# The convolution of branch A started two units earlier with its norm behind it, and the residual for the memory stage rebuilt

## The chip, the cores and the metric

The kernel runs on one core of a Trainium2 chip. The metric is the time of one execution in device microseconds, from the first to the last instruction of that core with what lies around it. TensorE (PE; its weight loads are shown as PEld), VectorE (DVE), ScalarE (ACT), GpSimd (POOL) and the queue that issues the transfers (SP) run side by side, each through its own list of instructions in order.

## The reference, cut to what matters

One layer over 256 tokens of width 1024, in fp32:

```python
h = layer_norm(x, ln0_g, ln0_b)
z = h @ w_in + b_in                       # 13 parts: a_val, a_gate, b_*, c_*, d_*, g_merge
u = a_val * sigmoid(a_gate)                                   # branch A
y_a = silu(layer_norm(causal_depthwise_conv(u, conv_a_w, conv_a_b), ln_a_g, ln_a_b))
...                                       # y_b: gated linear attention, y_c: stick-breaking, y_d: RG-LRU
proj   = einsum("bsnc,ncd->bsnd", stack([y_a, y_b, y_c, y_d]), w_branch)
merged = sum(sigmoid(g_merge) * proj, over the four branches)
h = layer_norm(ALPHA * h + merged @ w_out + b_out, ln1)
h = layer_norm(ALPHA * h + cross_attention(h, mem), ln2)
h = layer_norm(ALPHA * h + moe(h), ln3)   # 32 experts, top 4, w1 1024x2048, w2 1024x1024 each
```

The convolution of branch A has 31 taps over 512 channels, so each token needs the 30 before it. Its norm runs over the 512 channels.

## The kernel before, in words

All weights of the layer ahead of the experts come as tiles of 1 MB, and each tile is one **unit** of work. A unit is loaded by a transfer that SP issues, split into a high part (cast by ACT, L162) and a low part (the remainder, 5/16 of it on POOL, L164, and 11/16 on DVE, L166), and multiplied on PE in three passes (high by high, high by low, low by high; L135, L137, L139). There are two raw buffers and three split ones, so a raw buffer is free for the next load when both parts of the low half are done, and the split of unit i+3 needs unit i to be done on PE. `step` issues one unit at a time and splits two units ahead.

Units are counted from 0 here. 0 to 3 are the value and gate of branch A; 4 to 9 the queries, keys and values of branch C (4 and 7 queries, 5 and 8 keys, 6 and 9 values); 10 to 19 are for branches B and D. Then come gates and branch projections, in the order of branches C, B, D, A: 20 to 25 for C, 26 to 31 for B (29 and 30 are gates, 28 and 31 projections), 32 to 37 for D, and for A the gates 38 to 41 and the projections 42 and 43. 44 is the first tile of `ca_wk` (keys of the memory), 45 to 48 are `w_out`.

What is not a unit is a **chain**: a generator that `advance` moves on twice in every step, once before the unit's first half and once before its second half. So what a chain issues stands in each engine's list at that place, and the list is fixed when the program is built. The chains that the change touches:

- `chain_conv`: the convolution, 124 taps on DVE (L377 the first of a block of 128 channels, L379 the others), each over 128 x 256 numbers in SBUF. It starts ahead of unit 4, two taps at each advance.
- `chain_a`: the norm of branch A. Sums over the channels on PE with a matrix of 1/512 (L389 `ps_am` the mean, L396 `ps_av` the variance), the rest on DVE and ACT, and last `ysplit(0, ca)`, which casts `y_a` to `yh[0]` on ACT (L128) and puts the remainder in `yl[0]` on DVE (L129). PE needs `yh[0]` and `yl[0]` in units 42 and 43. It is appended ahead of unit 38.
- `chain_mem`: loads the memory (1 MB), `x` again (1 MB) and three rows broadcast to all partitions (0.5 MB each), splits the memory for units 44 and on, and builds ALPHA * LN(x) + b_out in `h`, to which units 45 to 48 add their products. The normalization runs on DVE (L861), gain and bias on POOL (L862, L864), the last step on DVE (L868). It is also appended ahead of unit 38.

Two buffers hold `yh` and two `yl`, given out in the order of branches C, B, D, A; so `yh[0]` takes the one of branch B, which unit 31 reads last. The PSUM tiles of units 4 to 19 come from a pool of two: unit 6 needs that of unit 4, which DVE empties with L422 (`qc`), and unit 8 that of unit 6, emptied with L433 (`vc`).

Behind the units come attention to the memory, routing, and the experts (w1 and w2 are 12.6 MB each expert, 402.7 MB in all), whose loads run through the freed buffers.

## Time and profile before

| | |
|---|---|
| median of three runs | 1424.52 us (1424.35 to 1425.74) |
| the profiled execution | 1425.04 us, of which the span of the instructions is 1423.3 us |
| PE busy | 1261.5 us (89%) |
| DVE busy | 522.1 us (37%) |
| ACT busy | 314.4 us (22%) |
| POOL busy | 231.2 us (16%) |
| transfers | 482.04 MB, mean 339 GB/s |

All times below are microseconds from the start of the span. Shares of the whole span say little, since it has two parts: up to some 480 us the units and chains, and from there the experts. A row of a timeline gives start and duration of one group of equal instructions in a row, and in brackets how long the engine sat idle before it and which instruction released it.

### The profile page before, as it was taken

How to read it: one execution, taken by the hardware profiler on the slowest of the kernel's cores; microseconds unless marked ns; L12 is line 12 of the kernel's file. 1: busy time of each engine (PE TensorE's matmuls, PEld its weight loads, DVE VectorE, ACT ScalarE, POOL GpSimd, SP SyncE). 2: the span in 40 equal slices, each digit the busy share in tenths (PEclk: the TensorE clock that was granted, in tenths of full speed). 3: DMA queues.
4: the chain of work that ended last, by engine and by line, in shares of the span. 5: the costliest groups of instructions: out<-in, count | busy, mean ns of one | idle time of the engine just before them, and what ended most of it. 6: DMA issues, size and time to landing. Idle time of an engine off the chain costs nothing. (4 is left out here: it accounts for less than half of the span.)

```text
span 1423.3 us, 18504 instructions
## 1 busy us (share of the span) xinstructions
PE 1261.5 (89%) x7677; PEld 743.5 (52%) x7677; DVE 522.1 (37%) x814; ACT 314.4 (22%) x433; POOL 231.2 (16%) x143
## 2 busy tenths in 40 slices
PE   6999999989999999876999799799889987977764
PEld 6989898988999743321443343244244332322211
DVE  5587779977944621211121121111112211211113
ACT  4475574453643300000000000000000000000001
POOL 6233234559653200000000000000000000000000
PEclk9999999998999999998999999999999999998988
DMA  6353334566565999999999999999999999999995
GB/s 235 119 177 121 119 119 154 187 237 191 195 258 206 387 424 407 424 424 425 427 424 426 424 424 427 425 426 425 424 425 426 426 423 424 425 427 426 425 420 240
DMA packets 51979, 482.04 MB, mean 339 GB/s; under 512 B 7840, under 2 KB 8240, under 8 KB 10704
## 3 DMA queue, kind: packets, MB, share of 16 engines
q1 hardware_dynamic: 51888, 480.79, 82.8%
q8 instruction: 62, 1.02, 0.3%
q14 instruction: 29, 0.24, 0.0%
HBM read 479.72 MB, written 1.05 MB: 338 GB/s over the span
## 5 line engine op out<-in xcount | busy, mean ns | idle before, releaser
L1471 PE MATMUL ps_h<-w,xg 128*32 128x512 f32 (+2 forms) x2048 | 419.0, 640 | 69.7 <-DMA w<-in_moe_w 65.8
L1471 PEld LDWEIGHTS ps_h<-w,xg 128*32 128x32 f32 (+2 forms) x2048 | 132.7, 134 | 331.6 <-issue 217.5
L1534 PE MATMUL ps_y<-w,at 128*32 128x512 f32 (+2 forms) x1024 | 213.5, 628 | 36.3 <-DMA w<-in_moe_w 34.5
L1480 DVE TENSOR_SCALAR act<-ps_h 128x512 f32<-128x512 f32 (+1 forms) x36 | 24.7, 687 | 503.6 <-PE ps_h L1471 503.6
L164 POOL TENSOR_TENSOR w_hl<-w_f,w_hl 128x640 fp32r<-128x640 f32 (+1 forms) x64 | 160.9, 2518 | 228.5 <-ACT w_hl L162 214.3
L1676 POOL TENSOR_TENSOR r<-r,gb 128x512 f32<-128x512 f32 x2 | 3.0, 1491 | 923.4 <-ACT r L1675 923.4
L1534 PEld LDWEIGHTS ps_y<-w,at 128*32 128x32 f32 (+2 forms) x1024 | 62.7, 133 | 165.5 <-issue 84.8
L166 DVE TENSOR_TENSOR w_hl<-w_f,w_hl 128x1408 fp32r<-128x1408 f32 x63 | 118.6, 1885 | 70.6 <-ACT w_hl L162 69.5
L162 ACT CAST w_hl<-w_f 128x2048 fp32r<-128x2048 f32 x63 | 119.9, 1905 | 104.6 <-DMA w_f<-in_w_in 35.2
L1518 ACT COPY ta<-ps_sc 128x256 f32<-128x256 f32 x31 | 11.6, 373 | 453.5 <-PE ps_sc L1516 453.5
L379 DVE SCALAR_TENSOR_TENSOR convacc<-u,cols,convacc 128x256 f32<-128x256 f32 x120 | 89.7, 747 | 2.5
L135 PE MATMUL ps_mm<-hT_hi,w_hl 128*128 128x256 f32 x512 | 75.5, 291 | 5.2 <-ACT hT_hi L311 2.1
L139 PE MATMUL ps_mm<-hT_hi,w_hl 128*128 128x256 f32 x512 | 73.1, 286 | 2.6 <-POOL w_hl L164 1.9
L137 PE MATMUL ps_mm<-hT_lo,w_hl 128*128 128x256 f32 x512 | 73.9, 288 | 0.0
L135 PEld LDWEIGHTS ps_mm<-hT_hi,w_hl 128*128 128x128 f32 x512 | 67.5, 195 | 8.2 <-issue 3.1
L1552 PE MATMUL acc<-y,ta 64*128 64x512 f32 (+1 forms) x248 | 69.3, 611 | 1.3
L139 PEld LDWEIGHTS ps_mm<-hT_hi,w_hl 128*128 128x128 f32 x512 | 67.0, 194 | 3.2 <-POOL w_hl L164 2.3
L137 PEld LDWEIGHTS ps_mm<-hT_lo,w_hl 128*128 128x128 f32 x512 | 67.6, 196 | 0.6 <-DVE hT_lo L314 0.6
L1342 PEld LDWEIGHTS ps_g<-sg,h 128*128 128x128 f32 x416 | 53.0, 207 | 13.1 <-issue 9.1
L1342 PE MATMUL ps_g<-sg,h 128*128 128x128 f32 x416 | 55.5, 295 | 0.3
L1481 ACT ACTIVATE sg<-act 128x512 f32<-128x512 f32 (+1 forms) x36 | 22.7, 631 | 134.8 <-DVE act L1480 134.2
L1541 ACT COPY y<-ps_y 128x512 f32<-128x512 f32 x28 | 16.4, 587 | 160.7 <-PE ps_y L1534 160.7
(398 smaller groups left out, 1246.9 us busy)
## 6 DMA issues: line engine op xcount, KB each, us to landing
w<-in_moe_w SPq DMA_DIRECT2D x128, 2048.0 KB, 29.4
w<-in_moe_w SPq DMA_DIRECT2D x128, 1024.0 KB, 29.5
w_f<-in_w_in SPq DMA_DIRECT2D x36, 1024.0 KB, 4.9
w_f<-in_w_branch SPq DMA_DIRECT2D x8, 1024.0 KB, 4.9
w_f<-in_ca_wk SPq DMA_DIRECT2D x4, 1024.0 KB, 5.0
w_f<-in_w_out SPq DMA_DIRECT2D x4, 1024.0 KB, 5.0
w_f<-in_ca_wq SPq DMA_DIRECT2D x4, 1024.0 KB, 5.0
w_f<-in_ca_wv SPq DMA_DIRECT2D x4, 1024.0 KB, 5.1
```

The lines of the kernel that those rows point to most:

```text
L135: PE.matmul(out, wh(i), xh(i), start=first and i == ks[0], stop=False)
L137: PE.matmul(out, wh(i), xl(i), start=False, stop=False)
L139: PE.matmul(out, wl(i), xh(i), start=False, stop=last and i == ks[-1])
L162: A.copy(hi, self.raw)
L164: G.tensor_tensor(lo[:, :n], self.raw[:, :n], hi.bitcast(F32)[:, :n], ALU.subtract)
L166: V.tensor_tensor(lo[:, n:], self.raw[:, n:], hi.bitcast(F32)[:, n:], ALU.subtract)
L379: V.scalar_tensor_tensor(ca[:, c, :], u[:, c, j:j + T], col("caw", 4 * j + c), ca[:, c, :], ALU.mult, ALU.add)
L1342: PE.matmul(pss[k // 4][:, k % 4 * w:(k % 4 + 1) * w], h[:, n, feature_tile(0, k)], sg[:, n, :w], start=n == 0 and k % 4 == 0, stop=n == N ...
L1471: PE.matmul(up_out(cap, hp_, m, i), x[:, k, :], w[:, c:c + 512], start=False, stop=k == KD - 1, skip_group_check=True)
L1480: V.tensor_scalar(g, hg, LIMIT, None, ALU.min)
L1534: PE.matmul(o, at[:, k, :], w[:, q * 512:(q + 1) * 512], start=k < (2 if cap == 32 else 1), stop=k >= KD - (2 if cap == 32 else 1), skip_g ...
L1552: PE.matmul(acc[n][q], a, b, start=False, stop=last, skip_group_check=True)
```

## The change

Three parts. The convolution starts ahead of unit 2, four taps at each advance until unit 7 and two from there, and `chain_a` follows as soon as the taps are issued; its last step waits, when the program is built, until unit 31 has been issued. The residual is built with `c0 = ALPHA * b0 + b_out` (one DVE step) and per token tile `(x - mean) * g0` and `* (ALPHA * rstd) + c0` (two DVE steps), with nothing on POOL. The transfers of `chain_mem` are issued at three advances, between weight loads, instead of one.

```diff
-    taps_per_step = 2
-
     def chain_conv():
...
-                if n % taps_per_step == 0:
+                if n >= (4 if st_["done"] < 7 else 2):
+                    n = 0
                     yield
+        yield from chain_a()
...
+        while not (wb_done and 3 in yh):
+            yield
         ysplit(0, ca)
...
+            if (n, hf) == (1, 1):
+                wb_done.append(1)
...
     chains.append(chain_b0())
+    conv[0] = chain_conv()
+    chains.append(conv[0])
     until(4)
     pms[:] = [(pmm, "mm")]
-    conv[0] = chain_conv()
-    chains.append(conv[0])
     until(7)
...
     def chain_mem():
         S.dma_start(mf, t["memT"])
+        yield
         S.dma_start(h, xrow)
-        g0, b0, bo = bcast("ln0_g"), bcast("ln0_b"), bcast("b_out")
+        g0 = bcast("ln0_g")
         for q in range(4):
-            yield
             yield
             sl = slice(2 * q, 2 * q + 2)
             split(mf[:, sl, :], mTh[:, sl, :], mTl[:, sl, :])
-            if q < 2:
-                V.tensor_scalar(h[:, q, :], h[:, q, :], *mr0[q], ALU.subtract, ALU.mult)
-                G.tensor_tensor(h[:, q, :], h[:, q, :], g0, ALU.mult)
+            yield
+            if q == 0:
+                b0 = bcast("ln0_b")
+                c0 = bcast("b_out")
+            elif q < 3:
+                n = q - 1
+                mean, rstd = mr0[n]
+                V.scalar_tensor_tensor(h[:, n, :], h[:, n, :], mean, g0, ALU.subtract, ALU.mult)
+                V.tensor_scalar(rstd, rstd, ALPHA, None, ALU.mult)
             else:
-                G.tensor_tensor(h[:, q - 2, :], h[:, q - 2, :], b0, ALU.add)
-        yield
+                V.scalar_tensor_tensor(c0, b0, ALPHA, c0, ALU.mult, ALU.add)
         for n in range(NT):
             yield
-            V.scalar_tensor_tensor(h[:, n, :], h[:, n, :], ALPHA, bo, ALU.mult, ALU.add)
+            V.scalar_tensor_tensor(h[:, n, :], h[:, n, :], mr0[n][1], c0, ALU.mult, ALU.add)
...
-    chains.append(chain_a())
     chains.append(chain_mem())
```

What this does to the lists of the engines is shown at three places. The first is DVE from the low part of unit 3 to `qc`, which empties the PSUM tile of unit 4. `u` is the input of the convolution (L276), `lr`, `e1`, `b16` and `e3` belong to branch B, and the `w_hl` tiles are the low parts of the weights. Before:

```order
L129 TENSOR_TENSOR wlr_lo_191<-wlr_190,wlr_hi_192 128x128
L166 TENSOR_TENSOR w_hl_359<-w_f_295,w_hl_359 128x1408
L505 TENSOR_SCALAR lr_437<-ps_lr_412,cols_82 16x256
L166 TENSOR_TENSOR w_hl_441<-w_f_357,w_hl_441 128x1408
L276 SCALAR_TENSOR_TENSOR u_198<-ps_mm_363,cols_82,a_sg_494 128x256 x2
L513 TENSOR_SCALAR e1_211<-ps_ga_499,cols_82 128x256 x2
L377 TENSOR_SCALAR convacc_200<-u_198,cols_82 128x256
L379 SCALAR_TENSOR_TENSOR convacc_200<-u_198,cols_82,convacc_200 128x256
L166 TENSOR_TENSOR w_hl_512<-w_f_439,w_hl_512 128x1408
L379 SCALAR_TENSOR_TENSOR convacc_200<-u_198,cols_82,convacc_200 128x256 x2
L422 TENSOR_SCALAR qc_204<-ps_mm_516,cols_82 128x256 x2
```

The same place of the changed kernel, from the first taps on (its lines 376 and 378 are the taps, 277 is `u`, 509 and 517 are `lr` and `e1`, 426 is `qc`):

```order
L376 TENSOR_SCALAR convacc_200<-u_198,cols_82 128x256
L378 SCALAR_TENSOR_TENSOR convacc_200<-u_198,cols_82,convacc_200 128x256 x3
L166 TENSOR_TENSOR w_hl_363<-w_f_295,w_hl_363 128x1408
L378 SCALAR_TENSOR_TENSOR convacc_200<-u_198,cols_82,convacc_200 128x256 x4
L509 TENSOR_SCALAR lr_445<-ps_lr_420,cols_82 16x256
...
L166 TENSOR_TENSOR w_hl_453<-w_f_361,w_hl_453 128x1408
...
L277 SCALAR_TENSOR_TENSOR u_198<-ps_mm_367,cols_82,a_sg_510 128x256 x2
L517 TENSOR_SCALAR e1_211<-ps_ga_515,cols_82 128x256 x2
...
L166 TENSOR_TENSOR w_hl_530<-w_f_451,w_hl_530 128x1408
...
L426 TENSOR_SCALAR qc_204<-ps_mm_534,cols_82 128x256 x2
```

Each row of "..." in this piece stands for four taps (line 378). So 16 taps now stand between the low-rank weights and `u`, where there were none, and eight between `e1` and `qc`, where there were four. Behind `qc` the changed list has 16 taps up to `vc`, which empties the tile of unit 6; before there were eight.

The second place is PE where the sums of the norm now stand: `w_hl_2300` is unit 29, `w_hl_2362` unit 30, `w_hl_2426` unit 31.

```order
L139 MATMUL ps_mm_2430<-hT_hi_91,w_hl_2300 128x256 x8
L391 MATMUL ps_am_2485<-convacc_200,ones_165 128x256 x4
L135 MATMUL ps_mm_2498<-hT_hi_91,w_hl_2362 128x256 x8
L137 MATMUL ps_mm_2498<-hT_lo_90,w_hl_2362 128x256 x8
...
L398 MATMUL ps_av_2550<-u_2484,ones_165 128x256 x4
L135 MATMUL ps_mm_2566<-yh1_2040,w_hl_2426 128x256 x4
```

On DVE the last taps, on which `ps_am` waits, stand at this place of the changed list (line 776 takes the product of unit 28, line 392 takes the mean off; `w_hl_2426` is the low part of unit 31):

```order
L776 TENSOR_TENSOR gate_2355<-ps_mm_2395,gate_2355 128x512
L378 SCALAR_TENSOR_TENSOR convacc_200<-u_198,cols_82,convacc_200 128x256 x2
L166 TENSOR_TENSOR w_hl_2426<-w_f_2360,w_hl_2426 128x1408
...
L392 TENSOR_TENSOR convacc_200<-convacc_200,ps_am_2485 128x1024
L166 TENSOR_TENSOR w_hl_2494<-w_f_2424,w_hl_2494 128x1408
```

There "..." stands for two more taps, the last of the convolution. Before, two taps, the low part of unit 31 and two taps stood behind the product of unit 28 as well, more taps followed up to unit 37, and the sums stood on PE ahead of unit 38 and ahead of its successor 39.

The third place is SP's list, from the load of unit 40 to that of unit 43. Before:

```order
L151 DMA w_f_2894<-in_w_in 128x2048
L852 DMA memT_f_2963<-in_memT 128x2048
L853 DMA h_2965<-in_x 128x2x1024
L843 DMA bc_ln0_g_2978<-in_ln0_g 128x1024
L843 DMA bc_ln0_b_2980<-in_ln0_b 128x1024
L843 DMA bc_b_out_2982<-in_b_out 128x1024
L151 DMA w_f_2984<-in_w_in 128x2048
L151 DMA w_f_3056<-in_w_branch 128x2048
L151 DMA w_f_3124<-in_w_branch 128x2048
```

And in the changed kernel:

```order
L858 DMA memT_f_2991<-in_memT 128x2048
L151 DMA w_f_2997<-in_w_in 128x2048
L860 DMA h_2993<-in_x 128x2x1024
L849 DMA bc_ln0_g_3029<-in_ln0_g 128x1024
L151 DMA w_f_3060<-in_w_branch 128x2048
L849 DMA bc_ln0_b_3091<-in_ln0_b 128x1024
L849 DMA bc_b_out_3093<-in_b_out 128x1024
L151 DMA w_f_3124<-in_w_branch 128x2048
```

The load of unit 41 had five transfers of 3.5 MB ahead of it; now it has the memory's 1 MB, unit 42 has 1.5 MB and unit 43 has 1 MB.

## Rows read from the trace of the kernel before

**Rows 1.** Expert stage by stretch: us, PE, PEld, DVE, ACT, POOL busy, clock, DMA share, GB/s.
```profile
485.00:1400.00 915.00, 800.62 (x4074) 308.49 (x4076) 160.10 (x328) 63.19 (x120) 4.97 (x3) 0.95 1.01 424
```

**Rows 2.** Timeline of PE, units 6 and 8: start, us, line, op, count, idle before, releaser.
```profile
58.03 1.19 PE L135 MATMUL ps_mm<-w_hl,hT_hi 128*128 128x256 f32 x8 [1.10 <-DVE qc L422]
...
72.55 1.18 PE L135 MATMUL ps_mm<-hT_hi,w_hl 128*128 128x256 f32 x8 [1.50 <-DVE vc L433]
```

**Rows 3.** Timeline of DVE, 32 to 72 us.
```profile
32.80 1.63 DVE L166 TENSOR_TENSOR w_hl<-w_f,w_hl 128x1408 fp32r<-128x1408 f32 x1 [1.28 <-ACT w_hl L162]
...
38.46 0.47 DVE L505 TENSOR_SCALAR lr<-ps_lr,cols 16x256 f32<-16x256 f32 x1 [4.03 <-PE ps_lr L139]
...
44.72 0.88 DVE L276 SCALAR_TENSOR_TENSOR u<-ps_mm,cols,a_sg 128x256 f32<-128x256 f32 x2 [3.94 <-ACT a_sg L275]
...
53.24 1.62 DVE L166 TENSOR_TENSOR w_hl<-w_f,w_hl 128x1408 fp32r<-128x1408 f32 x1 [5.38 <-ACT w_hl L162]
...
60.39 1.00 DVE L379 SCALAR_TENSOR_TENSOR convacc<-u,cols,convacc 128x256 f32<-128x256 f32 x2
...
63.28 1.62 DVE L166 TENSOR_TENSOR w_hl<-w_f,w_hl 128x1408 fp32r<-128x1408 f32 x1 [1.89 <-ACT w_hl L162]
...
71.72 0.68 DVE L433 TENSOR_TENSOR vc<-ps_mm,bb 128x512 f32<-128x512 f32 x1
```

**Rows 4.** Timeline of POOL, 53 to 75 us.
```profile
53.29 3.01 POOL L164 TENSOR_TENSOR w_hl<-w_f,w_hl 128x640 fp32r<-128x640 f32 x1 [13.99 <-ACT w_hl L162]
...
73.32 1.84 POOL L164 TENSOR_TENSOR w_hl<-w_f,w_hl 128x640 fp32r<-128x640 f32 x1 [5.28 <-ACT w_hl L162]
```

**Rows 5.** Timeline of DVE, the one tap beside the first of these.
```profile
54.79 1.79 DVE L379 SCALAR_TENSOR_TENSOR convacc<-u,cols,convacc 128x256 f32<-128x256 f32 x1
```

**Rows 6.** Timeline of PE, unit 30 and the start of unit 31.
```profile
239.85 1.12 PE L135 MATMUL ps_mm<-hT_hi,w_hl 128*128 128x256 f32 x8
...
245.61 0.64 PE L135 MATMUL ps_mm<-yh,w_hl 128*128 128x256 f32 x4
```

**Rows 7.** Timeline of DVE, one tap at 249 us.
```profile
248.75 0.48 DVE L379 SCALAR_TENSOR_TENSOR convacc<-u,cols,convacc 128x256 f32<-128x256 f32 x1
```

**Rows 8.** Busy time by stretch, 230 to 250 us (columns as in Rows 1).
```profile
230.00:250.00 20.00, 19.88 (x167) 19.68 (x166) 19.43 (x19) 8.74 (x10) 11.10 (x6) 1.00 0.54 188
```

**Rows 9.** Timeline of PE, the column sums as they stand now, and unit 38.
```profile
286.40 1.89 PE L389 MATMUL ps_am<-convacc,ones 128*128 128x256 f32 x8
287.94 1.30 PE L135 MATMUL ps_mm<-hT_hi,w_hl 128*128 128x256 f32 x8
```

**Rows 10.** Timeline of PE, a wait at 147 us.
```profile
146.90 0.99 PE L588 MATMUL ps_kv<-vb,ket 64*64 64x128 f32 x16 [2.77 <-DVE yl L129]
```

**Rows 11.** Busy time and granted clock by stretch, behind that wait (columns as in Rows 1).
```profile
148.00:151.40 3.40, 3.40 (x17) 3.40 (x17) 3.26 (x9) 0.00 (x0) 0.00 (x0) 0.50 0.32 135
```

**Rows 12.** Timeline of PE, units 42 and 43 and the start of unit 44.
```profile
316.45 0.74 PE L135 MATMUL ps_mm<-yh,w_hl 128*128 128x256 f32 x4 [2.17 <-ACT yh L128]
319.89 1.22 PE L137 MATMUL ps_mm<-yl,w_hl 128*128 128x256 f32 x4 [2.71 <-DVE yl L129]
...
325.64 0.64 PE L137 MATMUL ps_mm<-yl,w_hl 128*128 128x256 f32 x4
...
333.68 1.10 PE L135 MATMUL ps_mm<-memT_hl,w_hl 128*128 128x256 f32 x8
```

**Rows 13.** Timeline of PE, unit 45 (first of w_out) and the start of unit 46.
```profile
344.10 0.80 PE L135 MATMUL ps_mm<-w_hl,merged_hl 128*128 128x256 f32 x2 [1.00 <-ACT merged_hl L128]
...
351.54 1.12 PE L135 MATMUL ps_mm<-w_hl,merged_hl 128*128 128x256 f32 x8
```

**Rows 14.** Timeline of DVE, one residual step.
```profile
332.35 1.39 DVE L868 SCALAR_TENSOR_TENSOR h<-h,bc_b_out 128x1024 f32<-128x1024 f32 x1
```

**Rows 15.** Timeline of POOL, one residual step.
```profile
315.08 3.68 POOL L862 TENSOR_TENSOR h<-h,bc_ln_g 128x1024 f32<-128x1024 f32 x1 [4.94 <-DVE h L861]
```

**Rows 16.** Timeline of ACT, the cast of unit 41.
```profile
305.17 1.91 ACT L162 CAST w_hl<-w_f 128x2048 fp32r<-128x2048 f32 x1 [6.64 <-DMA w_f<-in_w_in]
```

More of the change, by code (lines that the diff above doesn't have):

```diff
@@ L261, in hybrid_layer_kernel @@
     gates = {}
+    wb_done = []
     first_merge = []
```

## Prediction

> **What bounds the kernel now.** I read the shares in slices first: from some 485 us to 1400 us the transfers run at 424 GB/s with no gap [rows 1], so there the experts' loads set the pace. No instruction of that stage changes; its loads wait for buffers that the units before it free, so a microsecond gained or lost ahead of 480 us should move the whole stream, and the end, by one. Then the timeline of PE up to 480 us: it works nearly without a break, and what counts is each place where it waits. For such a place I looked at the engine named and then at what stood before it in that engine's list.
>
> The change touches three such places: the waits of units 6 and 8 [rows 2], a stretch at 230 to 250 us where PE does not wait but DVE is busy for 19.43 of 20 us [rows 8], and the long break ahead of units 42 and 43 [rows 12], with the one of unit 45 behind it [rows 13].
>
> **The early taps (loss).** A tap costs 0.52 us in a series (0.48 and a gap) [rows 3]. Beside POOL's part of a split it costs more: POOL's instruction at 53.29 us took 3.01 us, while DVE's half of that split ran for 1.62 us first [rows 3, 4], and the tap behind took 1.79 us [rows 5], 1.3 us over its 0.48. So the first tap behind waits until POOL is done, and POOL needs some 1.45 us alone; the taps after it run at 0.52 again. The Trainium skill says so ("SBUF — State Buffer", Who interferes with whom): a DVE instruction with two SBUF inputs and a GpSimd one that reads SBUF exclude each other for the whole instruction. Were the port shared out evenly instead, each of the 28 extra taps might cost some 1.1 us (half way between 0.48 and 1.79), and this term would be up to 12 us larger; the single tap and the pair of 1.00 us speak for the lock.
>
> From 32 us to `u` of unit 3 DVE stood idle for 1.28 + 4.03 + 3.94 = 9.25 us [rows 3]. Into that go 16 taps, 8.3 us, and two halts for POOL, 2.9 us: 2.0 us too much. Part of one halt lies beside a split that waits for POOL today as well, so I put `u` 1.4 us later than now. Behind it `e1`, the logarithm on ACT and the cast of unit 6 move by as much, so DVE's part of unit 6 starts at 54.6 us in place of 53.24. Two more taps behind that, 1.0 us: `qc` and unit 6 come 2.4 us later, and PE's idle time before unit 6 grows from 1.1 to 3.5 us.
>
> From `qc` to `vc` there are 16 taps in place of eight: 4.2 us. Two of them fit into the 1.89 us that DVE waits there now for the cast of unit 7 [rows 3]; six, 3.1 us, do not. POOL's part of unit 9, which now starts 1.6 us behind `vc` (73.32 against 71.72) [rows 3, 4], would fall ahead of `vc`, since its weights do not come as much later as `vc` does: one more halt, 1.5 us. So unit 8 comes 2.4 + 3.1 + 1.5 = 7.0 us later, and its idle time grows from 1.5 to 6.1 us. From unit 8 on both lists are the same up to the sums, so PE keeps this. Lower bound: 1.0 us, if only the two taps ahead of `qc` counted; upper bound 9 us, if one more halt fell in each of the two places. I take 7.0, since each term has its row.
>
> **The clock (loss).** After 2.77 us idle at 147 us [rows 10] the granted clock was 0.50, the lower level of 1.2 GHz, for the 3.4 us from 148.0 to 151.4 [rows 11]: 1.7 us of work lost. After 2.17 and 2.71 us idle ahead of unit 42, the seven groups of four products from 319.89 to 325.64 us took 5.75 us [rows 12]; the next 17 took 8.04, 0.473 us each, so 2.4 us were lost. Idle times of 3.5 and 6.1 us are longer than these, so I put 1.7 and 2.2 us, 3.9 in all. Bounds 0 (1.5 us idle ahead of unit 8 now costs nothing that I can see) and 5.
>
> **The norm behind the convolution (loss).** The mean's product now stands ahead of unit 30, half a step behind the last two taps. What matters is how far DVE is behind there. PE starts unit 30 at 239.85 us [rows 6]. The taps at the same place of DVE's list, two behind the low part of unit 31, run only until 249.2 us (the second is the row at 248.75) [rows 7]: DVE works a unit and a half behind PE. Today that is harmless, since splits are issued two units ahead. But the product needs the last tap. So PE would stand from about 240 to 249.2 us, then do the last quarter: unit 30 starts near 249.7 us, 9.85 later than now. The product itself, 1.54 us (286.40 to 287.94) [rows 9], only changes its place, as does that of the variance. Loss 8.3 us, and behind such a break again 2.2 us at the lower clock: 10.5. Bounds: 0, if DVE had caught up by then, and 11.9, if the clock stays low longer, as in the 6.6 us behind the break of unit 42. Nothing hides it: all that PE could do instead stands behind it in its list. The rest of `chain_a` then finds DVE nearly level with PE: seven groups of steps spread over four units, from which 28 taps (14.6 us) have gone. I cost it at nothing; DVE's splits hide behind the two units of lead that the break rebuilds.
>
> **What the norm's new place removes (gain).** Units 38 to 43 now take from 287.94 to 333.68 us, 45.74 us [rows 9, 12]. Four gates at 5.76 us (unit 30: 239.85 to 245.61) [rows 6], the variance's product at 1.6 us and 24 groups at 0.473 us come to 36.0 us. So 9.7 us are lost now: the waits for `yh` and `yl` [rows 12], the slow clock behind them, and a shorter wait at unit 41, whose cast stood 6.64 us for its transfer behind the 3.5 MB [rows 16]. With `y_a` split some 50 us earlier and the loads apart all of it could go. The next thing late is a weight tile: unit 42 comes behind 1.5 MB and unit 43 behind 1 MB, 3.5 and 2.4 us at 424 GB/s [rows 1], while the 8.3 us of the 3.5 MB cost PE no more than the wait at unit 41; so I count no wait for weights. Gain 9.7, at worst 5.
>
> Unit 45 waits for the merged branches: from the start of unit 44 to that of unit 46 17.86 us pass [rows 12, 13], against 11.52 for two units and 0.6 for a small product; 5.7 us are lost, part of it at the low clock behind the break (the wait shown is the last of two). DVE has a step more there (`c0`, by the last step of today 1.39 us [rows 14]), but POOL no longer holds steps of the residual such as the 3.68 us one [rows 15], which also slow DVE. I take 4.3 us, leaving a wait of 1.5 us too short to bring the clock down; bounds 0 and 5.7.
>
> **The residual.** DVE gets two steps and a bit more, POOL loses four steps of some 2.4 to 3.7 us [rows 15]; both lie beside units 39 to 43 and neither is waited for but in the term above.
>
> **The sum.** Against the profiled execution, 1425.04 us with a span of 1423.3: + 7.0 + 3.9 + 10.5 - 9.7 - 4.3 = + 7.4, that is 1432.4 us; the median of the runs is 0.5 lower, so **1431.9 us**. Its own range, with the clock and the first wait at half or at their upper bounds, is 1426 to 1437 us.
>
> **Rivals.** First, faster: DVE is level with PE at the mean's product. Then the 10.5 us go, and the sum is - 3.1: 1421.4 us. The place is the break ahead of unit 30, and the change is faster as soon as that break costs less than 3.1 us. For it: PE's waits at units 6 and 8 give DVE time. Against: DVE's list between unit 8 and unit 28 is the same as now, so whatever puts it behind today is still there.
>
> Second, faster too: the early taps fit into idle time of DVE, and units 6 and 8 wait no longer than now; without 10.9 us the sum is - 3.5, 1421.0 us. For it speak 9.25 us idle, against it that `qc` and `vc` are late already [rows 2].
>
> Third, slower still: the weights take the place of `y_a` as what is late at units 41 to 43. If 2.5 MB of small transfers delay PE as 3.5 MB delayed the cast, 6.64 x 2.5 / 3.5 = 4.7 us, and unit 45 gains nothing, the sum is 7.4 + 4.7 + 4.3: 1440.9 us. For it: the load of unit 42 sits behind two transfers at once. Against: only one split stood out in the trace with all five ahead.
>
> Fourth, losses and gains cancel: half the loss at unit 30 and no slow clock early, 7.4 - 5.2 - 3.9 = - 1.7, within 0.2% (2.8 us, about what a measurement of this kernel tells from no change).
>
> **Chances.** Forecast 0.60, first rival 0.12, second 0.07, third 0.11, fourth 0.10. Faster by more than 0.2%: the first two, 0.18; within: the fourth and the lower edge of the forecast, 0.13; slower 0.69. For 8 in 10 the range goes from 1420 us, under the two faster rivals' sums, to 1440 us, short of the third's.
>
> **What would show it.** Right: PE idle 3 to 4 us before unit 6 and 5 to 6 us before unit 8, waiting for `qc` and `vc`; PE idle for 6 us or more on the mean's product, released by a tap; granted clock 0.5 behind these; no wait for `yh` or `yl` ahead of unit 42; the experts' stream at the same rate and as much later as the end. Wrong: the mean's product running without a wait, a cast waiting for its transfer at units 41 to 43, or an end that moves by less than the units do.

## The result and the profile after

The changed kernel takes 1434.77 us (median of four runs, 1432.39 to 1436.34), the kernel before 1425.13 us on the same chip: a ratio of 1.0068, 95% interval 1.0056 to 1.0080, so 9.6 us slower. The forecast was 1431.9 us.

The profiled execution took 1433.96 us with a span of 1432.3 us, 9.0 us longer than before. The expert stage runs at the same rate as in [rows 1]; here is its line (columns as there):

```profile
485.00:1400.00 915.00, 800.19 (x4100) 312.39 (x4099) 165.35 (x353) 67.39 (x125) 5.24 (x4) 0.96 1.01 424
```

So most of the time was lost ahead of it (the last column but one of the table below leaves 2.3 us of the 9.0 to what follows unit 58). The timeline of PE after shows where (start, duration, line, count; in brackets the idle time before and its releaser):

```profile
59.51 2.04 PE L135 MATMUL ps_mm<-w_hl,hT_hi 128*128 128x256 f32 x8 [2.74 <-DVE qc L426]
...
78.10 2.05 PE L135 MATMUL ps_mm<-hT_hi,w_hl 128*128 128x256 f32 x8 [4.34 <-DVE vc L437]
...
245.76 1.46 PE L391 MATMUL ps_am<-convacc,ones 128*128 128x256 f32 x6
253.88 1.22 PE L391 MATMUL ps_am<-convacc,ones 128*128 128x256 f32 x2 [6.66 <-DVE convacc L378]
254.54 2.27 PE L135 MATMUL ps_mm<-hT_hi,w_hl 128*128 128x256 f32 x8
...
347.56 0.50 PE L135 MATMUL ps_mm<-w_hl,merged_hl 128*128 128x256 f32 x2 [2.37 <-ACT merged_hl L128]
349.23 0.80 PE L135 MATMUL ps_mm<-w_hl,merged_hl 128*128 128x256 f32 x2 [1.18 <-ACT merged_hl L128]
...
359.61 2.08 PE L137 MATMUL ps_mm<-w_hl,merged_hl 128*128 128x256 f32 x8 [2.71 <-POOL w_hl L164]
```

The first two rows answer to [rows 2]: the waits grew from 1.10 and 1.50 us, and the eight products behind them take 2.04 and 2.05 us in place of 1.19 and 1.18: the clock fell (granted clock 0.50 from 59.5 to 61.5 us). The next three rows are the mean's product and what follows it: the profile shows each of its four matrix products as two, six of these eight run at once, the last two wait 6.66 us for the last channel's taps. Ahead of unit 42 the waits of [rows 12] are gone. The wait for the merged branches is still there, 2.37 + 1.18 us ([rows 13] show the last of two before). The last row is a wait that the kernel before does not have: unit 46 stands for POOL's part of its own split. The timeline of POOL has that split behind the sums of the merged branches and the constants for the routing, which begin with L1115 and run without a break up to it:

```profile
345.59 2.94 POOL L777 TENSOR_TENSOR merged<-merged,gate 128x512 f32<-128x512 f32 x2 [1.76 <-DVE gate L776]
348.49 1.06 POOL L1115 TENSOR_TENSOR rwg<-rw,cols 128x256 f32<-128x256 f32 x1
...
357.49 3.59 POOL L164 TENSOR_TENSOR w_hl<-w_f,w_hl 128x640 fp32r<-128x640 f32 x2
```

The granted clock around the end of that break (columns as in [rows 1]) is 0.52, about the lower level, 1.2 GHz in place of 2.4:

```profile
249.80:256.60 6.80, 2.72 (x10) 2.54 (x11) 5.21 (x5) 0.21 (x1) 1.63 (x1) 0.52 0.36 124
```

To compare kernels I took from PE's timeline the start of units 5, 10, 29, 38, 44, 46, 47 and 59 and the end of the span. The differences are what each stretch costs PE, waits and clock included (us; the last column is the median of the timed runs; the kernels are explained below):

| kernel | 5-9 | 10-28 | 29-37 | 38-43 | 44-45 | 46 | 47-58 | rest | median |
|---|---|---|---|---|---|---|---|---|---|
| before | 37.05 | 146.03 | 53.84 | 45.74 | 17.86 | 6.14 | 86.33 | 979.29 | 1425.1 |
| after | 43.91 | 145.24 | 63.77 | 34.39 | 17.62 | 10.07 | 84.84 | 981.61 | 1434.8 |
| early taps only | 44.20 | 145.12 | 53.59 | 42.71 | 16.38 | 7.12 | 86.26 | 980.28 | 1428.4 |
| norm two units later | 43.70 | 145.27 | 55.64 | 34.38 | 18.53 | 6.92 | 86.64 | 979.48 | 1422.9 |
| memory's chain only | 37.25 | 145.91 | 54.25 | 39.07 | 15.16 | 6.85 | 86.33 | 979.86 | 1421.0 |
| memory's chain old | 43.32 | 143.85 | 64.70 | 40.53 | 17.95 | 6.00 | 86.50 | 980.76 | 1436.2 |
| loads only | 37.07 | 145.25 | 54.25 | 37.24 | 23.83 | 12.46 | 84.59 | 981.49 | 1428.0 |
| constants later | 43.58 | 145.27 | 65.30 | 34.38 | 17.67 | 6.54 | 89.98 | 979.08 | 1437.1 |
| three taps, units 9-16 | 37.04 | 148.08 | 59.29 | 34.39 | 17.38 | 8.03 | 86.43 | 980.02 | 1422.3 |
| 16 early taps | 37.47 | 145.92 | 55.92 | 34.39 | 20.30 | 5.76 | 86.28 | 981.34 | 1418.9 |
| after, residual late | 43.54 | 145.27 | 65.13 | 34.39 | 12.14 | 10.34 | 84.62 | 981.31 | 1429.3 |
| memory only, residual late | 37.16 | 145.26 | 54.33 | 41.98 | 12.20 | 6.98 | 86.28 | 981.09 | 1416.3 |
| 16 taps, residual late | 37.62 | 145.07 | 55.86 | 34.38 | 13.65 | 12.71 | 84.62 | 980.36 | 1416.5 |
| and constants split | 37.64 | 145.07 | 56.08 | 34.39 | 13.80 | 8.49 | 94.76 | 980.27 | 1421.1 |

Where the norm stands early, its variance's product (1.6 us) has moved from column 38-43 to column 29-37, and nothing else changes its column.

### The profile page after: what moved, and what is told of

Same layout as the page of the kernel before. It is cut to its first block, busy times and chain, and to the rows that moved or that the text cites. A ratio compares the mean times of both kernels' runs of the same rounds, so it can differ in the third digit from the quotient of the medians.

```text
span 1432.3 us, 18504 instructions
## 1 busy us (share of the span) xinstructions
PE 1261.0 (88%) x7677; PEld 745.0 (52%) x7677; DVE 519.4 (36%) x817; ACT 314.7 (22%) x433; POOL 221.7 (15%) x139
## 5 line engine op out<-in xcount | busy, mean ns | idle before, releaser
L166 DVE TENSOR_TENSOR w_hl<-w_f,w_hl 128x1408 fp32r<-128x1408 f32 x63 | 114.4, 1818 | 80.6 <-ACT w_hl L162 80.5
L1529 ACT COPY ta<-ps_sc 128x256 f32<-128x256 f32 x31 | 11.5, 372 | 450.1 <-PE ps_sc L1527 450.1
L378 DVE SCALAR_TENSOR_TENSOR convacc<-u,cols,convacc 128x256 f32<-128x256 f32 x120 | 85.7, 714 | 2.7
```

The source lines that it names most:

```text
L166: V.tensor_tensor(lo[:, n:], self.raw[:, n:], hi.bitcast(F32)[:, n:], ALU.subtract)
L378: V.scalar_tensor_tensor(ca[:, c, :], u[:, c, j:j + T], col("caw", 4 * j + c), ca[:, c, :], ALU.mult, ALU.add)
```

## Experiments

**Early taps only.** The kernel before, with the new tap loop and its earlier start; norm and memory's chain as before.

```
-                if n % taps_per_step == 0:
+                if n >= (4 if st_["done"] < 7 else 2):
+                    n = 0
                     yield
...
+    conv[0] = chain_conv()
+    chains.append(conv[0])
     until(4)
```

> The kernel before with one part of the change: the taps from unit 2 on, four to a step until unit 7, two after that; the norm and the memory's chain stay where they were. Theory A (the early taps cost what the trace after shows): unit 8 starts 5.5 us later than before, PE waits about 2.7 us for qc and 4.3 us for vc, the clock falls to 0.5 behind each, units 9 to 37 run 5.8 us late, and since the waits ahead of unit 42 hang on the norm and not on the taps the end keeps most of it: 1430 to 1431 us. Theory B (the time comes back, since the last tap stands four units earlier and DVE has less to do at units 33 to 41, so that the norm's steps and the split of y_a come sooner): the waits ahead of units 42 and 43 shrink by as much, and the time is that of before, 1425 us.

1428.38 us (1.0014, 1.0004 to 1.0024): between the two. The early loss is as in the whole change, the waits are 2.78 and 4.42 us. But units 38 to 45 took 4.5 us less. The norm keeps its place in the lists in this run; what moved is the last tap, seven units forward, at 255.3 us in place of 287.0. With no taps left beside it the norm runs sooner behind PE: PE starts unit 38 6.1 us later than before, and the cast of y_a comes only 2.6 us later (317.93 against 315.36 us). So early taps cost 6 us at once, and about half of it returns at the seam, as long as the waits for y_a and the merged branches are there to shrink.

**Norm two units later.** The changed kernel, with PE given two units of other work between the last tap and the mean's product.

```
+        for _ in range(4):
+            yield
         yield from chain_a()
```

> The changed kernel with four more empty steps, that is two units, between the last tap and the norm's first product; everything else as changed. Theory A (the break ahead of unit 30 is DVE's arrears of a unit and a half, and PE's two further units cover them): no wait on ps_am over 0.5 us, no fall of the clock there, 8.8 + 2.7 = 11.5 us less, y_a still split ahead of unit 42: about 1423.3 us. Theory B (DVE only catches up because PE stands still, so the arrears last as long as PE works, and the break just moves two units on): PE waits 5 us or more at the product's new place and the time is within 3 us of the changed kernel, 1432 to 1435 us.

1422.88 us (0.9983, 0.9973 to 0.9993): theory A, 11.9 us less than the changed kernel. That this is so near to the 11.5 expected is in part luck: by the table 8.1 us of it lie at units 29 to 37, where the break was, and 3.2 at unit 46, of which the expectation says nothing. The timeline of PE shows all eight products of the mean in one piece, without a wait:

```profile
257.30 1.89 PE L393 MATMUL ps_am<-convacc,ones 128*128 128x256 f32 x8
```

So DVE's arrears at that place were a bounded amount that two units cover, and did not need PE's standstill to clear. The break was the largest single loss of the change.

**Memory's chain only** and **memory's chain old** split the change the other way: the first is the kernel before with the new `chain_mem`, the second the changed kernel with the old one (the first's edit is shown; the second's is its reverse).

```
         S.dma_start(mf, t["memT"])
+        yield
         S.dma_start(h, xrow)
-        g0, b0, bo = bcast("ln0_g"), bcast("ln0_b"), bcast("b_out")
+        g0 = bcast("ln0_g")
...
+                V.scalar_tensor_tensor(h[:, n, :], h[:, n, :], mean, g0, ALU.subtract, ALU.mult)
...
```

> The kernel before with the other part alone: the memory's chain of the changed kernel (residual in two DVE steps per token tile, loads spread out); convolution and norm as before. Theory A (what the trace after shows: DVE's steps with two SBUF inputs beside POOL's splits take about 2.6 us each and hold back the gates' products, and POOL's constants then stand ahead of the split of the unit behind unit 45): nothing changes up to unit 41, the waits ahead of unit 42 are no shorter, unit 45's wait does not shrink and the next unit waits 2 us more: 1426 to 1429 us. Theory B (my prediction's term): the wait for the merged branches shrinks by 4.3 us: 1421 us.

> The changed kernel with the memory's chain of the kernel before (all its loads at once, the residual's steps on POOL); taps and norm as changed. With the memory's chain alone, units 38 to 45 took 54.2 us, with the whole change 52.0, before 63.6. Theory A (the memory's chain makes that gain, not the earlier split of y_a): they take 58 us or more here, and the time is 1438 to 1441 us. Theory B (my prediction: the split of y_a, some 50 us earlier, makes most of it, and the chain only the last 4 us): they take 53 to 56 us, 1434 to 1437 us.

1420.95 us (0.9963, 0.9949 to 0.9977) and 1436.23 us (1.0083, 1.0066 to 1.0100). Theory A of the first run, which I had formed from the changed kernel's trace, falls: the chain alone shortens units 38 to 45 by 9.4 us. Its time is theory B's, but not by B's term: units 44 and 45 gain 2.7 us and units 38 to 43 the other 6.7. The second run lies between its theories: those units take 58.5 us, as A had it, but the time is in B's range. With 1.6 us for the moved product, convolution and norm alone bring 3.5 us at the seam, the chain alone 9.4, and both 10.0. So the two overlap. Of the gain that I had put down to the early split of `y_a`, the memory's chain makes most in either order of counting: 9.4 us alone, 6.5 on top of the other two parts. In medians, each against the kernel before that was run beside it, the chain is worth 4.9 us alone (1.8 on top of the others), and convolution and norm cost 11.5 to 14.5.

**Loads only.** Which part of the chain? The kernel before, with loads and splits at the new steps and the residual's arithmetic as it was.

```
+            if q == 0:
+                b0, bo = bcast("ln0_b"), bcast("b_out")
+            elif q < 3:
+                n = q - 1
+                V.tensor_scalar(h[:, n, :], h[:, n, :], *mr0[n], ALU.subtract, ALU.mult)
+                G.tensor_tensor(h[:, n, :], h[:, n, :], g0, ALU.mult)
...
```

> The kernel before with the memory's loads and splits at the steps of the changed kernel, but the residual computed as before, by DVE and POOL (products and sums of POOL at the same steps). Theory A (what gains in the memory's chain is the loads lying apart, so that the casts of units 41 to 43 do not wait for their transfers): no cast waits over 2 us there, units 38 to 45 take 54 to 57 us, 1419 to 1422 us. Theory B (what gains is POOL's relief from the residual): they take 60 us or more, 1424 to 1427 us.

1428.03 us (1.0021, 1.0011 to 1.0031): neither theory by itself, though theory B's figures are the nearer ones (61.1 us for units 38 to 45). Spreading the loads takes 8.5 us out of units 38 to 43, and then units 44 to 46 give 12.3 us back. The timeline of POOL in this run says why:

```profile
312.24 3.31 POOL L866 TENSOR_TENSOR h<-h,bc_ln_g 128x1024 f32<-128x1024 f32 x1 [0.63 <-DVE h L865]
...
319.81 2.77 POOL L866 TENSOR_TENSOR h<-h,bc_ln_g 128x1024 f32<-128x1024 f32 x1 [2.28 <-DVE h L865]
...
325.47 4.74 POOL L869 TENSOR_TENSOR h<-h,bc_ln_b 128x1024 f32<-128x1024 f32 x2
330.16 4.86 POOL L773 TENSOR_TENSOR merged<-merged,gate 128x512 f32<-128x512 f32 x2
...
351.93 3.04 POOL L164 TENSOR_TENSOR w_hl<-w_f,w_hl 128x640 fp32r<-128x640 f32 x2
```

The residual's steps (L866, L869, as in [rows 15]) now stand right ahead of the sums of the merged branches, and unit 46's split waits behind them all. So the loads free units 38 to 43, and taking the residual off POOL lets units 44 to 46 keep it. By themselves the spread loads cost 3.3 us against the kernel before that was run beside them, and with the rewritten residual the chain gains 4.9. What the rewritten residual is worth with the loads as before was not tried; nor was this residual with its two last steps on POOL (L869) further apart.

**Constants later.** The changed kernel, with POOL's constants for the routing (some 9 us from L1115 on) behind unit 46's split, at the price of three more half steps in their chain.

```
         o = _COLS["ln2g"]
+        yield
         G.tensor_tensor(rwg, rwf, ...
...
+        yield
+        yield
         G.iota(tie[:, :NE], ...
```

> The changed kernel with POOL's constants for the routing put half a unit (to aident) and a unit and a half (the rest) further back in its list, so that the split for the second unit of w_out stands ahead of them. Theory A (that split, and with it PE, waited for the constants): the wait of 2.08 to 2.7 us there goes, with the clock behind it 3.7 us, and the time falls to about 1431 us. Theory B (PE's wait is set by the cast or by the transfer, not by POOL's list, or the constants hit the next split as hard): unit starts from there on shift by under 1 us, 1434 to 1435 us.

1437.14 us (1.0082, 1.0065 to 1.0099). Unit 46 takes 3.5 us less, as theory A has it, but units 47 to 58 take 5.1 us more: the norm behind w_out waits 2.73 us for `h` and 2.13 us for `rgb`, the last step of the chain that I had made longer. The wait was real, its removal was no gain, and the time lies above both theories.

**Residual late.** The changed kernel, with the sum of biases and the residual's last two steps behind the splits of the merged branches, and its first two steps two half steps earlier.

```
-            elif q < 3:
-                n = q - 1
+            if q < 2:
+                n = q
...
-            else:
-                V.scalar_tensor_tensor(c0, b0, ALPHA, c0, ALU.mult, ALU.add)
+        while not mem_end:
+            yield
+        V.scalar_tensor_tensor(c0, b0, ALPHA, c0, ALU.mult, ALU.add)
...
     until(NMIX)
+    mem_end.append(1)
```

> The changed kernel with the residual's steps elsewhere in DVE's list: the two steps with mean and gain one to three half steps earlier, the sum of biases and the last two steps behind the splits of the merged branches instead of ahead of the last gates' products. In the changed kernel the product of unit 43's gates started at 344.83 us, behind two residual steps of 2.6 us. Theory A (these steps, slowed beside POOL, are what cost my gain at unit 45, and by POOL's list the wait at the next unit too): unit 43's product starts 4 us earlier, the waits of 3.5 us for the merged branches and of 2.08 us for POOL's split go to under 1 us each, and the time falls to 1427 to 1430 us. Theory B (the merged branches are late because PE, without breaks, arrives earlier, and DVE's and POOL's splits alone hold them): the waits shrink by under 1.5 us, 1433 to 1435 us.

1429.30 us (1.0038, 1.0026 to 1.0050): theory A for the merged branches. In the changed kernel the timeline of DVE reads

```profile
334.10 2.59 DVE L877 SCALAR_TENSOR_TENSOR bc_b_out<-bc_ln_b,bc_b_out 128x1024 f32<-128x1024 f32 x1
336.61 1.27 DVE L776 TENSOR_TENSOR gate<-ps_mm,gate 128x512 f32<-128x512 f32 x2
337.81 1.94 DVE L880 SCALAR_TENSOR_TENSOR h<-h,l0rs,bc_b_out 128x1024 f32<-128x1024 f32 x1
339.67 2.72 DVE L166 TENSOR_TENSOR w_hl<-w_f,w_hl 128x1408 fp32r<-128x1408 f32 x1
342.32 2.59 DVE L880 SCALAR_TENSOR_TENSOR h<-h,l0rs,bc_b_out 128x1024 f32<-128x1024 f32 x1
344.83 1.27 DVE L776 TENSOR_TENSOR gate<-ps_mm,gate 128x512 f32<-128x512 f32 x2
```

and in this run the two products of the gates start at

```profile
333.31 1.28 DVE L776 TENSOR_TENSOR gate<-ps_mm,gate 128x512 f32<-128x512 f32 x2
...
339.06 1.28 DVE L776 TENSOR_TENSOR gate<-ps_mm,gate 128x512 f32<-128x512 f32 x2
```

The last gates' product (L776) comes 5.8 us earlier, and units 44 and 45 take 12.14 us: two units and a small product, with nothing lost. Unit 46's wait stayed, 3.07 us on POOL's split, so that half of theory A did not come. It hangs on POOL's constants, but not on them alone: at their new place the residual's last two steps run beside the constants and make two small steps of POOL take 1 us more each (the rows of the run with 16 early taps and the residual late, below, show the same). From the first constant to the split pass 9.4 us here, 9.0 in the changed kernel and 7.8 in the kernel before.

**Three taps at units 9 to 16.** The memory's chain with the norm moved forward by taps in the middle instead of at the start: the convolution starts ahead of unit 4, as before, and the norm stands one unit behind the last tap.

```
-                if n >= (4 if st_["done"] < 7 else 2):
+                if n >= (3 if 9 <= st_["done"] < 17 else 2):
...
+        for _ in range(2):
+            yield
         yield from chain_a()
```

> The kernel before with the changed memory's chain, two taps to a step from unit 4 as before, but three to a step from unit 9 to unit 16, and the norm one unit behind the last tap: the norm moves four to five units forward, at no cost to units 6 and 8. Against the run with the memory's chain alone (1420.95 us). Theory A (DVE has room between units 9 and 16, where it is busy for 14 to 16 of 20 us, and the remaining wait of 2.5 us for y_a ahead of unit 42 goes, with the low clock behind it): no wait on ps_am over 1 us, no new wait at units 9 to 20, 1417 to 1420 us. Theory B (the taps hold back the chains of branches B and C, or the norm meets DVE in arrears): PE waits 3 us or more at one of the two, 1423 us or more. Theory C (what y_a no longer costs is spent at the wait for the merged branches, which DVE and POOL set): unit 42 comes earlier and unit 46 does not, 1420 to 1422 us.

1422.29 us (0.9980, 0.9970 to 0.9989). PE waits 1.9 us at the mean's product and a little longer at units 10 and 17 than with the memory's chain only (columns 10-28 and 29-37: 2.2 and 5.0 us more, 1.6 us of the latter for the moved product); y_a's wait goes, but counted from unit 5 PE starts unit 42 5.1 us later than with the memory's chain only, and unit 46 4.5 us later. The time lies between those of theories B and C; the mechanism is B's at a smaller size, since in C unit 42 would have come earlier.

**16 early taps.** The changed kernel with four taps at each advance only until unit 4, and the norm two units behind the last tap.

```
-                if n >= (4 if st_["done"] < 7 else 2):
+                if n >= (4 if st_["done"] < 4 else 2):
...
+        for _ in range(4):
+            yield
         yield from chain_a()
```

> The changed kernel with the fast taps cut from 28 extra to 16: four to a step until unit 4 only, two from there on, and the norm two units behind the last tap. Theory A (the early loss is the taps that stand ahead of qc and vc in DVE's list; those ahead of unit 4 are only the ones that fit into DVE's idle time): units 6 and 8 come under 1.5 us later than before, no wait at the norm, and with the memory's chain 1418 to 1421 us. Theory B (the taps ahead of unit 4 hold back u, and with it all that follows): unit 6 still comes 1.5 us late or more and PE falls to the lower clock there, 1422 to 1426 us.

1418.88 us (0.9956, 0.9940 to 0.9973): theory A. Units 5 to 9 lose 0.4 us in place of 6.9. So the early loss belongs to the 12 taps at units 4 to 6, which stand ahead of `qc` and `vc`; the 16 ahead of unit 4 fit into DVE's idle time. PE reaches unit 44 early and then waits 4.7 us at unit 45 for the merged branches.

**The same with the residual late, and the memory's chain only with the residual late.**

> The run with 16 early taps and the norm two units later (1418.88 us), with the residual's steps moved in the same way. There unit 42's product of the gates started 5.7 us and unit 43's 8.1 us behind the end of its unit, and PE waited 4.7 us for the merged branches. Theory A (DVE's list ahead of the products is what PE waits for): the products start within 2 us, the wait goes to under 1 us, and with the clock behind it 4 to 6 us are gained: 1413 to 1415 us. Theory B (POOL's sums and splits hold the merged branches): under 1.5 us are gained, 1417 to 1419 us.

> The run with the memory's chain alone (1420.95 us), taps and norm as before, with the residual's steps moved in the same way. Theory A (as above, and y_a's split, at 314 us in the place behind the residual's first step, holds unit 42 by 2.5 us still): 1 to 3 us are gained, 1418 to 1420 us, and the run with the norm moved forward is 4 us ahead, which is then what the norm's place is worth. Theory B (without DVE's steps in between unit 42's wait goes too): 1414 to 1416 us, and the norm's place is worth nothing.

1416.46 us (0.9939, 0.9925 to 0.9952) and 1416.29 us (0.9938, 0.9925 to 0.9952), the two fastest. The first lies between its theories: the wait for the merged branches fell to 1.19 us, and unit 46 took 7 us more than without the edit. The second holds convolution and norm as before, and still waits 3.79 us for `y_a` in unit 42, as theory A says; its time, and that the norm's place is worth nothing, are theory B's. With the norm forward that wait goes, units 38 to 45 are 6.2 us shorter (4.6 without the moved product), and the end is the same. The gain is lost at unit 46, by the timelines of POOL, DVE and PE in the first of the two:

```profile
331.14 1.06 POOL L1119 TENSOR_TENSOR rwg<-rw,cols 128x256 f32<-128x256 f32 x1
...
334.41 2.44 POOL L1137 TENSOR_SCALAR_AFFINE_SELECT tie<-tie 32x1 f32<-32x1 f32 x2
336.91 1.16 POOL L1135 TENSOR_SCALAR tie<-tie 32x1 f32<-32x1 f32 x1
338.14 0.42 POOL L1137 TENSOR_SCALAR_AFFINE_SELECT tie<-tie 32x1 f32<-32x1 f32 x2
...
340.53 1.53 POOL L164 TENSOR_TENSOR w_hl<-w_f,w_hl 128x640 fp32r<-128x640 f32 x1
```

```profile
335.53 2.47 DVE L884 SCALAR_TENSOR_TENSOR h<-h,l0rs,bc_b_out 128x1024 f32<-128x1024 f32 x2
```

```profile
342.11 2.08 PE L137 MATMUL ps_mm<-w_hl,merged_hl 128*128 128x256 f32 x8 [3.98 <-POOL w_hl L164]
```

The constants run from 331.14 to 340.5 us, the split behind them, and PE behind that. Three of the small steps on `tie` took 1.13 to 1.24 us each, one while DVE ran its part of a split and two while it ran the residual's last steps, where the others took some 0.2 us. So moving the residual took part of the collision from DVE's list, ahead of the gates' products, to POOL's, ahead of unit 46's split: the constants took 9.4 us up to that split, 7.75 without the edit. How much of the 3.98 us of waiting would be left without it was not tried.

**And the constants split.** The first of these two, with the constants in two pieces behind the splits of units 46 and 47, in the half steps that their chain had already.

```
+        yield
         G.tensor_tensor(rwg, rwf, ...
...
         yield
-        yield
         ps = pax.tile([NE, 2], F32, tag="ax", name="ps_rs")
...
                 yield
+                if (rows, q) == (96, 0):
+                    G.iota(tie[:, :NE], ...
```

> The run with 16 early taps and the residual's steps moved (1416.46 us), with POOL's constants for the routing taken from ahead of the split for unit 46 and put in two pieces behind it and behind the next, with no step more in their chain (the earlier try with three steps more gave the time back at the norm behind w_out). There POOL's part of unit 46's split stood 7 us behind its cast, PE waited 4.0 us for it, and the loads behind it waited for its buffer. Theory A (POOL's list is what PE waits for at unit 46, and nothing else is near): that wait goes, units 47 to 59 come 4 to 6 us earlier, 1410 to 1413 us. Theory B (the next is as late: the transfers of w_out or the mean of the norm behind it): unit 47 comes earlier, unit 54 by under 2 us, 1415 to 1417 us.

1421.07 us (0.9963, 0.9950 to 0.9976): theory B, and worse than it. Unit 47 starts 3.4 us earlier than without the edit. Ahead of it PE waited 2.58 us for its cast, which had stood 9.44 us for the transfer of `w_out`, as theory B names it. And the second piece of the constants, which took 7.4 us here (349.33 to 356.73 us) against 4.7 in the changed kernel, holds up POOL's splits of the units behind, and the chain runs on, by the timelines of POOL, SP, ACT and PE:

```profile
356.81 5.60 POOL L164 TENSOR_TENSOR w_hl<-w_f,w_hl 128x640 fp32r<-128x640 f32 x2
```

```profile
362.44 0.33 SPq L151 DMA_DIRECT2D w_f<-in_ca_wk  x1
```

```profile
365.17 1.90 ACT L162 CAST w_hl<-w_f 128x2048 fp32r<-128x2048 f32 x1 [4.65 <-DMA w_f<-in_ca_wk]
```

```profile
371.90 1.97 PE L235 MATMUL ps_tr<-ident,h 128*128 128x128 f32 x8 [5.53 <-DVE h L125]
```

The splits end at 362.4 us, only then a load of ca_wk is issued, its cast waits 4.65 us for it, DVE's part of that split stands in DVE's list ahead of the last part of `h`, and the norm waits 5.53 us. So POOL's constants cost something at each of the three places tried among these units. A place far ahead of them was not tried.

## Why the prediction was right, and where it was not

The direction, the places and the main mechanisms held; the measured terms (the table, after less before) stand beside those of the sum so:

- **Early taps and clock, 7.0 + 3.9 predicted, 5.9 measured.** Unit 8 starts 5.5 us later (78.10 against 72.55 us) in place of 7.0, and the clock behind it costs 2.1 us (from its start to that of its sixth group of eight products pass 6.9 us in place of 4.9), about the 2.2 of the sum. That the term as a whole came out smaller has four reasons.

  First, `u` came 0.44 us late and not 1.4. DVE was halted for POOL twice ahead of it, as I had it (three taps took 2.81 us and four 3.42 in the rows below; four alone take 2.04), but the 16 taps with both halts took 10.4 us in place of 11.2.

```profile
31.72 2.81 DVE L378 SCALAR_TENSOR_TENSOR convacc<-u,cols,convacc 128x256 f32<-128x256 f32 x3
35.99 3.42 DVE L378 SCALAR_TENSOR_TENSOR convacc<-u,cols,convacc 128x256 f32<-128x256 f32 x4
...
45.16 0.87 DVE L277 SCALAR_TENSOR_TENSOR u<-ps_mm,cols,a_sg 128x256 f32<-128x256 f32 x2
...
66.29 4.02 DVE L378 SCALAR_TENSOR_TENSOR convacc<-u,cols,convacc 128x256 f32<-128x256 f32 x3
...
74.17 3.19 DVE L378 SCALAR_TENSOR_TENSOR convacc<-u,cols,convacc 128x256 f32<-128x256 f32 x4
```

```profile
32.69 1.56 POOL L164 TENSOR_TENSOR w_hl<-w_f,w_hl 128x640 fp32r<-128x640 f32 x1 [3.64 <-ACT w_hl L162]
37.56 1.57 POOL L164 TENSOR_TENSOR w_hl<-w_f,w_hl 128x640 fp32r<-128x640 f32 x1 [3.31 <-DVE convacc L378]
...
64.79 4.71 POOL L164 TENSOR_TENSOR w_hl<-w_f,w_hl 128x640 fp32r<-128x640 f32 x2 [8.07 <-ACT w_hl L162]
74.86 1.69 POOL L164 TENSOR_TENSOR w_hl<-w_f,w_hl 128x640 fp32r<-128x640 f32 x1 [5.35 <-ACT w_hl L162]
```

  (The releaser at 37.56 us is no halt of POOL: ACT's cast for this split, from 35.57 us on for 1.91 us, ends 0.08 us before it, and in the kernel before the split follows its cast at the same distance.)

  Second, between `qc` and `vc` only one halt is new. The taps at 66.29 us meet two splits, but so do four taps of the kernel before (4.54 us); the new one is that of unit 9's split, as I had it, and took 1.15 us in place of 1.5.

  Third, the 1.7 us for the clock behind unit 6 should not have been in the sum at all. The products there did lose 1.2 us, but unit 8 waits for `vc`, which comes at DVE's time: in the changed kernel, with the clock at the lower level behind unit 6, unit 8 starts 18.59 us after unit 6, and in the run with the constants later, with the clock at the upper level there, 18.62 us. Only the idle time ahead of unit 8 is then 5.60 us and not 4.34.

```profile
59.07 1.19 PE L135 MATMUL ps_mm<-w_hl,hT_hi 128*128 128x256 f32 x8 [2.75 <-DVE qc L426]
...
77.69 2.05 PE L135 MATMUL ps_mm<-hT_hi,w_hl 128*128 128x256 f32 x8 [5.60 <-DVE vc L437]
```

  Fourth, two waits of the kernel before, for `c_ab`, fall away behind unit 8, worth 0.9 us each:

```profile
79.20 0.91 PE L475 MATMUL ps_z<-c_ab,ntri 128*128 128x384 f32 x2 [0.67 <-DVE c_ab L470]
...
94.65 0.91 PE L475 MATMUL ps_z<-c_ab,ntri 128*128 128x384 f32 x2 [0.66 <-DVE c_ab L470]
```

  So 5.5 + 2.1 - 1.8, and 0.1 more by unit 29.
- **Norm ahead of unit 30, 10.5 predicted, 8.3 measured** (63.77 - 53.84 = 9.9, less 1.6 for the variance's product that moved in). The mechanism is as put: the last two taps ran at 252.83 us and PE had to stand 6.66 us for them. DVE's arrears were 8.1 us against the 9.35 that I read from [rows 6, 7], so unit 30 was held 7.2 us and not 8.3, and the clock behind the break cost 1.2 us and not 2.2. The run with the norm two units later confirms the term as a whole: units 29 to 37 take 8.1 us less there.
- **Units 38 to 43, -9.7 predicted, -9.7 measured** (45.74 - 34.39 = 11.35, less the 1.6 us moved out). The size is right, and rival three, the weights, is out: PE waits for none there. The cause is only half right. I named the early split of `y_a` and the loads apart in one breath; the runs show that the loads alone bring 8.5 us of it, and convolution and norm alone 3.6 (45.74 - 1.6 - 40.53, with the memory's chain old).
- **Unit 45, -4.3 predicted, -0.2 measured: the step that failed.** I wrote that DVE has one step more there, at 1.39 us [rows 14], and that POOL's relief outweighs it. But DVE's new steps read two operands from SBUF, as the taps do, and met POOL's splits and sums: 2.59, 1.94 and 2.59 us in the rows above, not 1.39. The kernel before had shown this too: of its two last steps I took the one that was not held, and the other reads

```profile
336.31 2.31 DVE L868 SCALAR_TENSOR_TENSOR h<-h,bc_b_out 128x1024 f32<-128x1024 f32 x1
```

  And these three stood in DVE's list ahead of the gates' products on which the merged branches hang. I had used the slowing by POOL for the taps and not for the residual. With those steps elsewhere, units 44 and 45 fell by 5.5 us to 12.14. That the same chain without the early norm did gain there (15.16 us) does not contradict this, as I read it, though no run shows it: there PE still waited for `y_a` and reached unit 44 later (39.07 us for units 38 to 43 against 34.39), which gave DVE and POOL the time.
- **Unit 46, not in the sum, +3.9 measured.** POOL's list (sums of merged branches, constants, split) was what PE met there. I had looked at what POOL loses, the residual, and not at what it still holds.
- **Behind it** -1.5 us at units 47 to 58, and +2.3 us in the rest, which lies between 979.1 and 981.6 us in all these profiles without an order that I can see. What sets it stays open.

The sum of the measured terms is + 5.9 + 8.3 - 9.7 - 0.2 + 3.9 - 1.5 + 2.3 = + 9.0 us, against + 7.4 predicted: the losses early were 7.2 us smaller than thought [5.9 + 8.3 in place of 21.4], and the gain at unit 45 and the wait at unit 46 took 8.0 us in the other direction. So the time came out near the forecast partly by luck, because two errors met. Rivals one and two (DVE level with PE, early taps hidden) are out by the waits of 6.66, 2.74 and 4.34 us, rival four by the time, 0.68% and not within 0.2%. Of the signs that I had named, the waits ahead of units 6 and 8 came in the right places but smaller (2.74 and 4.34 us against 3 to 4 and 5 to 6).

## What to carry to other kernels

Before work is moved forward on an engine that runs behind, read how far behind it is at the new place, and leave so many units between its last step and the first product that needs it: two units were worth 8.1 us at that place here. When the waits of two units in a row hang on another engine's list, count the clock behind the last of them only: behind the first it shortens the next wait. When a wait is taken out of a chain of units, go through the lists of all the engines that feed the next ones, with everything that still stands in them; here a gain at units 38 to 43 was eaten up first by DVE's list at unit 45, then by POOL's at unit 46, then, in the runs that moved POOL's constants, by the norm behind it. And try the parts of a change alone: this one had a part worth 5 us (9 with its steps in a better place) inside a whole that cost 10.

## What was not expected of the hardware

An elementwise step of DVE with two operands in SBUF, of 128x1024, took 1.2 to 1.4 us where nothing held it and 2.59 us behind a POOL split; and the halt falls on whichever engine comes second, POOL included. It shows as a longer duration of the held instruction. The same split of POOL came 0.05 us behind DVE's own (32.80 us, [rows 3]) in the kernel before and took 3.01 us,

```profile
32.85 3.01 POOL L164 TENSOR_TENSOR w_hl<-w_f,w_hl 128x640 fp32r<-128x640 f32 x1 [3.63 <-ACT w_hl L162]
```

and in the changed kernel, at 32.69 us, it came just ahead of a tap and took 1.56 us, while the three taps took 2.81. Even steps of POOL on 32x1 numbers took 1.13 to 1.24 us in place of 0.2 beside such steps of DVE, so small setup work on POOL is not out of the way. The Trainium skill ("SBUF — State Buffer", Who interferes with whom) says that a DVE instruction with two SBUF inputs and a GpSimd one that reads SBUF exclude each other, and that the order of issue decides who is held. These rows agree with both.

The same idle time does not always bring the clock down: behind 2.74 to 2.78 us ahead of unit 6 the eight products took 2.04 or 2.05 us in the changed kernel and in the runs with the early taps only and with the memory's chain old, and 1.19 us in the runs with the constants later (its row stands above), the norm two units later and the residual late. The granted clock from 59.5 to 61.5 us was 0.50 in the changed kernel and 1.00 with the constants later. So a term for the clock behind a wait of 2 to 3 us, read from one place, is good to a microsecond and no better, and this one was worth 0.2 us at most: unit 8 starts 18.57 to 18.80 us after unit 6 in all six.
